# A hybrid encoder on one core: the recurrent mixer's score matmuls issued as one group, and the last cross-attention head's halves of the tokens in the other order

## The chip, the core and the metric

The kernel runs on one core of a Trainium2 chip, as one program. The metric is device time in microseconds of one execution. The core has a matrix engine (TensorE, PE in the views, with its weight loads as PEld), a vector engine (VectorE, DVE), an activation engine (ScalarE, ACT), a general engine (GpSimd, POOL) and SyncE (SP), which issues DMAs. Each engine works through its own stream of instructions in order; semaphores tie the streams together. SBUF is the on-chip working memory, PSUM holds the results of matmuls in eight banks of 128 × 512 float32.

## What is computed

Two layers over 1024 tokens of width 1024, all in float32. Each layer is a token mixer and a ConvGLU feed-forward, each between norms. Layer 0 mixes with windowed attention, layer 1 with a gated linear recurrence that runs forwards and backwards. Both mixers carry four cross-attention heads into 256 memory tokens. The part that the change touches, from the reference:

```python
def gla_chunked(q, k, v, log_f):            # one direction; chunks of HG_CHUNK tokens
    b = jnp.cumsum(log_f, axis=2)
    b_end = b[:, :, -1:]
    q_dec = q * jnp.exp(b)
    k_dec = k * jnp.exp(-b)
    k_end = k * jnp.exp(b_end - b)
    s = jnp.where(causal, jnp.einsum('bcthk,bcshk->bchts', q_dec, k_dec), 0.0)
    o_intra = jnp.einsum('bchts,bcshv->bcthv', s, v)
    def step(state, inp):
        qd, ke, vc, dec = inp
        o = jnp.einsum('bthk,bhkv->bthv', qd, state)
        state = dec[..., None] * state + jnp.einsum('bshk,bshv->bhkv', ke, vc)
        return state, o
...
    o = (gla_chunked(q, k_f, v, lf_f)
         + flip_t(gla_chunked(flip_t(q), flip_t(k_b), flip_t(v), flip_t(lf_b))))
    o = rmsnorm(o, norm_g.reshape(HG_HEADS, HG_VAL_DIM)).reshape(bsz, t, HG_W).astype(u.dtype)
    o = o * jax.nn.silu(gate)
    return jnp.concatenate([o, memory_cross_attn(xq, mem_kv)], axis=-1) @ w_out
```

There are 8 heads with keys and values of 128.

## The kernel before

**Stages.** `build` runs in this order: memory K/V for both layers and the first norm; `window` (layer 0's mixer); the output projection `WOut(0)`; `ffn(0)`; `hgrn` (layer 1's mixer); `WOut(1)`; `ffn(1)`. Every large product is three matmuls (`mm3`, `mmk`) on operands split into a high and a low part.

**Who sets the order.** The program is written with a framework whose planner decides, ahead of time, in which order each engine's instructions stand and which buffer a tile gets, from a simulated run of its own. Its preference is the order in which the kernel's code is written. `tc.high_priority(AHEAD)` lets what is written in its block rank as if it had been written `AHEAD` = 2000 instructions earlier. `tc.issue_after(ins)` puts the instructions of its block that run on the same engine behind `ins` in that engine's stream, without a wait for its end. On the chip each engine then follows its fixed stream.

**The recurrent mixer.** For each of the 8 heads `proj` makes q, the two forget inputs and, for two heads at a time, values and gates: long runs of projection matmuls into two PSUM banks (tag `pj`), 24 matmuls (8 input blocks, three each) for a bank. `head` then treats four directions: forwards over the first half of the tokens (d, b) = (0, 0), backwards over the second (1, 1), forwards over the second (0, 1), backwards over the first (1, 0). In the written order the projections of head h come before its directions and those of head h + 1 behind them.

`direction` makes decay factors on ScalarE, VectorE and GpSimd, with five buffers for the 128 × 512 tiles of tag `E` (E1, E2, and G for levels 32 and 64 among them) and two each for EP and ER. Scores within a 128-token chunk are made at three levels of blocks by `block` (line 1119): a matmul with 128 keys contracted, 32 stationary columns, 32 or 64 moving columns, and a place of its own among the array's columns. A direction has 8 calls at the 64-token level, 16 within blocks of 32 and 8 at the level of 32. `issue_after` puts the 24 others behind the first 8. All write the bank `pa[d]`. Behind them `copy_predicated` (line 1155) takes the valid scores out of `pa`, which go to As (line 1159 or 1161); ER is transposed (1164), copied to kT (1166), multiplied with v into the bank `pu` (1169), and the state S takes three or four steps on VectorE (1178) out of `pu`. The bank tags `po` and `pu` have one buffer each, `pt` has two.

`output` (for b = 1, then b = 0) sums scores times values and queries times states in `po` (1193), takes the mean square (line 100, ScalarE) and the root (line 93, GpSimd), scales into `on` (1199), transposes (1203), copies to `ot` (1205) and stores to `oT` in DRAM (1206).

**Cross-attention.** `cross` takes units (head, half of the tokens) from the list `units`, in places set by `HX`: two units each in heads 2, 4 and 6, behind the third and fourth direction, and in head 7 behind the second and third direction. The first unit of a head calls `cross_head`, which loads its keys and values and its query weights. `cross_unit` projects the query into `pj`, makes scores in `pt`, normalises, transposes, and accumulates the result in the bank `tags["po"][b]`: `po` for b = 0, `pu` for b = 1. It copies to `xo` (line 223), a tile that shares its one buffer with `ot`, and stores to `oT` from ScalarE's queue (224).

**The output projection** of layer 1 takes the token tiles in the order 4, 5, 6, 7, 0, 1, 2, 3. In head 7, behind the third direction's units, `wo1.early` begins tiles 4 and 5 with the heads that are done, in the two `pj` banks; `wo1.open` adds the last cross heads (reads of `oT`, line 453, split on line 86 and 87) and `finish` the last two recurrent heads, then the other tiles.

Of the kernel before, what the change touches and what calls it, by code (L numbers as in the profile page):

```python
# [16 lines left out]
P = 128  # L17
# [26 lines left out]
AHEAD = 2000  # L44


def build(tc, A, out):
# [130 lines left out]
    def cross_head(l, h, wp, raw):  # L178
        kvh = wp.tile([P, 2, 256], F32R, tag="kvh", bufs=1, name="kvh")
        kvl = wp.tile([P, 2, 256], F32R, tag="kvl", bufs=1, name="kvl")  # L180
        nc.sync.dma_start(raw, kvd[l][h])
        split(kvh, kvl, raw)
        return *wunit(A["wxq"][l, h]), kvh, kvl
# [755 lines left out]
    def hgrn():  # L939
# [5 lines left out]
        V, G = [late.tile([P, 3, NT, P], F32, name=x) for x in ("v", "gs")]  # L945
# [123 lines left out]
        def direction(h, r, d, b, qin, S, As):  # L1069
# [3 lines left out]
            lt, er = (0, 1) if d else (1, 0)  # L1073

            def E():
                return early.tile([P, 512], F32, tag="E", bufs=5, name="E")
# [24 lines left out]
            E1, E2 = E(), E()  # L1101
# [15 lines left out]
            def block(c, i, j, x, y, n=32):  # L1117

                return pe.matmul(pa[i:i + 32, c, j:j + n], x[:, c * P + i:c * P + i + 32], y[:, c * P + j:c * P + j + n],
                                 start=True, stop=True, tile_position=(0, i))  # L1120

            def step(n):
                pl_, pe_, rl_, re_ = parts(n)[:4]
                e = 0 if d else n - 1
                nb = 512 // (2 * n)
                dve.tensor_tensor(re_, re_, bc(pl_[:, :, e:e + 1], [P, nb, n]), op=ALU.mult)
                dve.tensor_tensor(pl_, pl_, bc(pe_[:, :, e:e + 1], [P, nb, n]), op=ALU.mult)  # L1127

            for n in (32, 64):
                step(n // 2)  # L1130
                G = E()
# [3 lines left out]
                dve.tensor_tensor(ge, re_, ke, op=ALU.mult)  # L1135
                if n == 32:
                    G32 = G
            for c in range(4):
                for o in (0, 32):
                    mm = block(c, er * 64 + o, lt * 64, G, G, 64)  # L1140
            with tc.issue_after(mm.ins):
                for c in range(4):
                    for o in range(0, P, 32):
                        block(c, o, o, E2, E1)
                for c in range(4):
                    for o in (0, 64):
                        block(c, o + er * 32, o + lt * 32, G32, G32)
            step(64)
            dec = wp.tile([P, 4], F32, tag="dec", bufs=2, name="dec")
            e = 0 if d else P - 1  # L1150
# [54 lines left out]
            act.activation(ot, tp, AF.Identity, scale=bng[:, h:h + 1])  # L1205
            nc.sync.dma_start(oT[1][h, :, b * 512:(b + 1) * 512], ot.rearrange("p c t -> p (c t)"))

        units = [(h, b) for h in range(4) for b in range(2)]
        xhead = [None]

        def cross(n):
            def pair(kind, i):
                return [wp.tile([P, 512], F32R, tag=kind + c, bufs=1, name=kind + c) for c in "hl"]

            for _ in range(n):
                xh_, xb_ = units.pop(0)
                if xb_ == 0:
                    raw = early.tile([P, 512], F32, tag="E", bufs=5, name="kv")
                    xhead[0] = cross_head(1, xh_, wp, raw.rearrange("p (a b) -> p a b", a=2))
                cross_unit(1, xh_, xb_, xhead[0], wp, tags, wp, pair)  # L1220

        def head(h, r):
            qin = [wp.tile([P, T], F32, tag=f"qin{d}", bufs=1, name="qin") for d in range(2)]
            S = [wp.tile([P, NT, P], F32, tag=f"S{d}", bufs=1, name="S") for d in range(2)]
            As = [None, None]
            for i, (d, b) in enumerate(((0, 0), (1, 1), (0, 1), (1, 0))):
                direction(h, r, d, b, qin[d], S[d], As)
                if i < len(r["later"]):
                    r["run"](r["later"][i])
                cross(HX[h][i])  # L1230
                if h == 7 and i == 2:
                    wo1.early(psj, 2, es)
            if h == 7:
                early.release()
                es.release()
                eq.release()
                wo1.open(2, 0)
            for i, b in enumerate((1, 0)):
                output(h, r, b, qin, S, As)
                cross(HX[h][4 + i])  # L1240
# [44 lines left out]
    wo0.finish()  # L1285
    ffn(0, wo0, h2d, True, (0, 1), (0, 1))
    hgrn()
    wo1.finish()
    ffn(1, wo1, out, False, (1, 0), (1, 0))
# [83 lines left out]
```

## Time and profile before

| | |
|---|---|
| median of 3 runs | 2715.87 us (2713.88 to 2719.8) |
| the profiled execution | 2715.91 us |
| its span, first to last instruction | 2714.1 us |
| mean granted TensorE clock | 0.992 |

| us from the start | what runs | TensorE busy |
|---|---|---|
| 0 to 250 | memory K/V, first norm, layer 0's mixer | 230.25 |
| 250 to 500 | layer 0's mixer | 233.07 |
| 500 to 1250 | output projection and feed-forward of layer 0 | 745.36 |
| 1250 to 1300 | start of the recurrent mixer | 48.86 |
| 1300 to 1900 | recurrent mixer | 588.74 |
| 1900 to 2000 | its end, output projection of layer 1 | 90.52 |
| 2000 to 2500 | output projection, feed-forward of layer 1 | 495.52 |
| 2500 to 2714.1 | feed-forward of layer 1 | 206.41 |

How to read the rows that follow. A row of the timeline has the start and the duration in us, the engine, the line of the kernel, the operation, output<-inputs by the program's names, the shape, the number of merged instructions, and in brackets the idle time of the engine ahead of it with what ended it. Matmuls are pipelined and their ends are modelled, so successive durations overlap; starts tell the pace. A `block` call leaves two records, since its operands are plain float32. A row of the view by stretches has from:to, the length, each engine's busy time with its instructions in the order PE, PEld, DVE, ACT, POOL, the granted TensorE clock, the DMA engines' share and GB/s.

### The profile page before, as it was taken

To read this page: it belongs to the slowest core of one execution; us is meant where nothing else is said; L and a number is where in the kernel's file an instruction comes from. 1 tells how busy PE (TensorE), PEld (TensorE's weight loads), DVE (VectorE), ACT (ScalarE), POOL (GpSimd) and SP (SyncE) were. 2 spreads that over 40 slices of the span, in tenths; PEclk is the share of its full clock that TensorE was granted. 3 is DMA by queue.
4 is the path that set the end of the run, shared out by engine and by line. 5 is a ranking of instruction groups with operands and counts; after the bars stand their busy time and mean duration, and the time that the engine had idled before them with its cause. 6 is when DMAs were issued, how large, how long until landed. Compare 5 with 4: busy or idle time off the path is not lost. (4 is left out here: it accounts for less than half of the span.)

```text
span 2714.1 us, 39502 instructions
## 1 busy us (share of the span) xinstructions
PE 2638.7 (97%) x14496; PEld 2204.5 (81%) x14496; DVE 1828.5 (67%) x3042; ACT 1391.6 (51%) x2556; POOL 468.4 (17%) x520
## 2 busy tenths in 40 slices
PE   8999999999999999999999999999899999999998
PEld 7888887788888888887877888878688788888887
DVE  6588787678565565487695768769567756566447
ACT  6367667545444444454454545545454544444443
POOL 1231110211111100031132222212121111110013
PEclk9999999999999999999999999999999999999999
DMA  7683213667777757673243432111476777775666
GB/s 284 209 179 84 60 52 100 188 190 181 210 197 196 205 149 255 195 256 124 69 150 106 111 88 67 52 51 34 125 219 174 188 209 206 202 201 155 226 194 233
DMA packets 215316, 432.25 MB, mean 159 GB/s; under 512 B 20561, under 2 KB 77265, under 8 KB 209489
## 3 DMA queue, kind: packets, MB, share of 16 engines
q1 hardware_dynamic: 188128, 335.07, 38.3%
q0 software_dynamic: 24544, 90.19, 15.9%
q10 hardware_dynamic: 2448, 4.46, 0.4%
q8 instruction: 114, 1.87, 0.3%
q14 instruction: 82, 0.66, 0.1%
HBM read 335.79 MB, written 117.96 MB: 167 GB/s over the span
## 5 line engine op out<-in xcount | busy, mean ns | idle before, releaser
L87 DVE TENSOR_TENSOR wl<-st,wh 128x1024 fp32r<-128x1024 f32 (+1 forms) x238 | 262.6, 1110 | 326.7 <-ACT wh L86 321.6
L86 ACT CAST wh<-st 128x1024 fp32r<-128x1024 f32 (+1 forms) x238 | 222.5, 937 | 295.9 <-PE X L535 195.9
L81 PE MATMUL pj<-uh,wh 128*128 128x512 f32 x512 | 205.2, 401 | 6.3 <-DVE xl L87 2.5
L535 PE MATMUL X<-wl,wh 128*128 128x512 f32 x528 | 204.8, 390 | 0.3 <-DVE wl L87 0.3
L535 PE MATMUL X<-wh,wl 128*128 128x512 f32 x528 | 204.6, 389 | 0.0
L82 PE MATMUL pj<-ul,wh 128*128 128x512 f32 x512 | 202.7, 396 | 0.1
L83 PE MATMUL pj<-uh,wl 128*128 128x512 f32 x512 | 202.2, 395 | 0.0
L535 PE MATMUL X<-wh 128*128 128x512 f32 x528 | 198.8, 390 | 1.4 <-ACT c L908 1.1
L81 PE MATMUL pj<-wh,uh 128*128 128x384 f32 (+1 forms) x512 | 190.4, 373 | 0.4 <-DVE v L280 0.4
L82 PE MATMUL pj<-wl,uh 128*128 128x384 f32 (+1 forms) x512 | 186.4, 364 | 0.0
L83 PE MATMUL pj<-wh,ul 128*128 128x384 f32 (+1 forms) x512 | 186.3, 365 | 0.0
L77 DVE TENSOR_TENSOR wl<-st,wh 128x1024 fp32r<-128x1024 f32 (+1 forms) x92 | 119.0, 1301 | 23.3 <-ACT wh L76 22.8
L535 PE MATMUL V<-uh,wh 128*128 128x512 f32 x344 | 133.8, 389 | 0.0
L535 PE MATMUL V<-ul,wh 128*128 128x512 f32 x344 | 133.8, 389 | 0.0
L535 PE MATMUL V<-uh,wl 128*128 128x512 f32 x344 | 133.8, 389 | 0.0
L76 ACT CAST wh<-st 128x1024 fp32r<-128x1024 f32 (+1 forms) x99 | 100.1, 1016 | 50.8 <-PE pj L82 31.0
L81 PEld LDWEIGHTS pj<-uh,wh 128*128 128x128 f32 x512 | 97.4, 190 | 26.7 <-DVE xl L87 2.9
L535 PEld LDWEIGHTS X<-wh 128*128 128x128 f32 x528 | 99.1, 188 | 22.8 <-ACT c L908 1.5
L535 PEld LDWEIGHTS X<-wl,wh 128*128 128x128 f32 x528 | 99.1, 188 | 21.0 <-DVE wl L87 0.7
L535 PEld LDWEIGHTS X<-wh,wl 128*128 128x128 f32 x528 | 99.1, 188 | 20.7
L1134 POOL TENSOR_TENSOR E<-EP,q 128x256 f32<-128x256 f32 x64 | 49.2, 769 | 372.3 <-DVE EP L1127 280.3
L83 PEld LDWEIGHTS pj<-uh,wl 128*128 128x128 f32 x512 | 97.0, 189 | 19.6
(347 smaller groups left out, 7274.4 us busy)
## 6 DMA issues: line engine op xcount, KB each, us to landing
st<-hid SPq DMA_DIRECT2D x154, 256.0 KB, 3.1
st<-in_ffw_dram SPq DMA_DIRECT2D x108, 256.0 KB, 3.1
w2s<-in_ffw_dram POOLq DMA_DIRECT2D x24, 1024.0 KB, 7.9
st<-in_ffw_dram SPq DMA_DIRECT2D x46, 512.0 KB, 4.1
hid<-tt SPq DMA_DIRECT2D x88, 256.0 KB, 4.6
st<-w2s SPq DMA_DIRECT2D x88, 256.0 KB, 3.3
sx<-in_ffw_dram SPq DMA_DIRECT2D x84, 256.0 KB, 3.9
sy<-in_ffw_dram SPq DMA_DIRECT2D x42, 512.0 KB, 6.3
```

Source lines behind the costliest of these rows:

```text
L76: act.copy(h[:, :n], raw)
L77: (eng or dve).tensor_tensor(l[:, :n], raw, h[:, :n].bitcast(F32), op=ALU.subtract)
L81: pe.matmul(o, ah, bh, start=first, stop=False)
L82: pe.matmul(o, ah, bl, start=False, stop=False)
L83: pe.matmul(o, al, bh, start=False, stop=last)
L86: act.copy(h, src)
L87: dve.tensor_tensor(l, src, h.bitcast(F32), op=ALU.subtract)
L535: pe.matmul(o, x, y, start=new, stop=e, skip_group_check=not first)
L1134: pool.tensor_tensor(gl, pl_, ql, op=ALU.mult)
```

## The change

The three loops over `block` go into a `high_priority` block as they are, `issue_after` included. And head 3 of the cross-attention, the last, takes its two halves of the tokens in the order 1, 0; `cross` finds the first unit of a head by a change of the head's number, no longer by b = 0.

```diff
-            for c in range(4):
-                for o in (0, 32):
-                    mm = block(c, er * 64 + o, lt * 64, G, G, 64)
-            with tc.issue_after(mm.ins):
+            with tc.high_priority(AHEAD):
                 for c in range(4):
-                    for o in range(0, P, 32):
-                        block(c, o, o, E2, E1)
-                for c in range(4):
-                    for o in (0, 64):
-                        block(c, o + er * 32, o + lt * 32, G32, G32)
+                    for o in (0, 32):
+                        mm = block(c, er * 64 + o, lt * 64, G, G, 64)
+                with tc.issue_after(mm.ins):
+                    for c in range(4):
+                        for o in range(0, P, 32):
+                            block(c, o, o, E2, E1)
+                    for c in range(4):
+                        for o in (0, 64):
+                            block(c, o + er * 32, o + lt * 32, G32, G32)
...
-        units = [(h, b) for h in range(4) for b in range(2)]
-        xhead = [None]
+        units = [(h, b) for h in range(4) for b in ((1, 0) if h == 3 else (0, 1))]
+        xhead = [None, None]
...
-                if xb_ == 0:
+                if xhead[1] != xh_:
+                    xhead[1] = xh_
                     raw = early.tile([P, 512], F32, tag="E", bufs=5, name="kv")
                     xhead[0] = cross_head(1, xh_, wp, raw.rearrange("p (a b) -> p a b", a=2))
```

## The prediction

> **What bounds the kernel now.** I read the page first, then busy time by stretches, then the groups of the changed line, then the TensorE timeline around it.
>
> ```profile
> span 2714.1 us, 39502 instructions
> PE 2638.7 (97%) x14496; PEld 2204.5 (81%) x14496; DVE 1828.5 (67%) x3042; ACT 1391.6 (51%) x2556; POOL 468.4 (17%) x520
> ```
>
> TensorE is busy for 97% of the span; no other engine is above 67%. The next view has, for a stretch of time, its length and each engine's busy time (with its instructions), then the granted clock and the DMA share:
>
> ```profile
> 1300.00:1900.00 600.00, 588.74 (x4664) 488.49 (x4666) 449.48 (x902) 308.12 (x675) 152.12 (x166) 0.99 0.29 82
> ```
>
> This stretch is the body of the recurrent mixer. In it TensorE idles 600 − 588.74 = 11.3 us, with VectorE at 449.48 / 600 = 75%. So there the end is set by how long TensorE needs for its stream of instructions, and what shortens that stream shortens the span. The score matmuls (`block`, line 1119) are part of it:
>
> ```profile
> L1119 PE MATMUL pa<-E x2048: 192/196/243, 1278.0 to 1919.2; 128*32 128x32 f32 x140, 128*32 128x64 f32 x47
> ```
>
> That is 32 directions (8 heads, 4 each) of 32 calls, 64 records a direction since a call leaves two. In the TensorE timeline these 2048 records stand in 73 unbroken runs, of which these are the first and the last:
>
> ```profile
> 1278.04 0.41 PE L1119 MATMUL pa<-E 128*32 128x64 f32 x6
> ...
> 1918.52 0.83 PE L1119 MATMUL pa<-E 128*32 128x64 f32 x52
> ```
>
> 19 directions are one run of 64. The other 13 are cut into 5, 3, 7, 3, 6, 5, 3, 6, 5, 3, 4, 2 and 2 runs (54 together), so there are 54 − 13 = 41 runs more than directions. One of the directions in five pieces, with the matmuls at its seams:
>
> ```profile
> 1615.25 0.39 PE L83 MATMUL pj<-wh,ul 128*128 128x512 f32 x1
> 1615.57 0.76 PE L1119 MATMUL pa<-E 128*32 128x64 f32 x26
> 1616.26 0.50 PE L81 MATMUL pj<-wh,uh 128*128 128x512 f32 x1
> 1616.59 0.39 PE L82 MATMUL pj<-wl,uh 128*128 128x512 f32 x1
> 1616.82 0.40 PE L83 MATMUL pj<-wh,ul 128*128 128x512 f32 x1
> ...
> 1621.92 0.32 PE L1119 MATMUL pa<-E 128*32 128x32 f32 x12
> 1622.17 0.50 PE L81 MATMUL pj<-wh,uh 128*128 128x512 f32 x1
> ...
> 1627.84 0.27 PE L1119 MATMUL pa<-E 128*32 128x32 f32 x8
> 1628.03 0.50 PE L81 MATMUL pj<-wh,uh 128*128 128x512 f32 x1
> ...
> 1633.70 0.32 PE L1119 MATMUL pa<-E 128*32 128x32 f32 x8
> 1633.95 0.50 PE L81 MATMUL pj<-wh,uh 128*128 128x512 f32 x1
> ...
> 1639.62 0.38 PE L1119 MATMUL pa<-E 128*32 128x32 f32 x10
> 1639.92 0.66 PE L1164 MATMUL pt<-ident,ER 128*128 128x128 f32 x4
> ```
>
> The durations overlap, so starts are compared. Two projection matmuls in a row start 0.23 us apart (1616.59 to 1616.82). A run is entered 0.32 after the matmul before it (1615.25 to 1615.57), 0.09 more. The first projection matmul behind it holds the engine 0.33 (1616.26 to 1616.59), 0.10 more. So each run pays about 0.19 us at its seams, besides its own length, and a direction in pieces pays that for each piece. A whole direction:
>
> ```profile
> 1397.16 0.39 PE L83 MATMUL pj<-uh,wl 128*128 128x512 f32 x1
> 1398.98 1.17 PE L1119 MATMUL pa<-E 128*32 128x64 f32 x64 [1.44 <-DVE s L1041]
> 1400.08 0.50 PE L81 MATMUL pj<-uh,wh 128*128 128x512 f32 x1
> ```
>
> **The change part by part.** *The score matmuls under high priority.* No instruction is added or removed; the order on TensorE changes. A direction's 32 calls now rank before about 2000 earlier instructions, so the planner should issue them together as soon as the last input G is ready, not in the gaps of the projection's stream.
>
> Price of a cut, from the rows above. From the run's start to the next other matmul: 0.69 + 0.25 + 0.19 + 0.25 + 0.30 = 1.68 for the five pieces, 1.10 for the whole run (1398.98 to 1400.08). With seams: 1.68 + 5 × 0.19 = 2.63 against 1.10 + 0.19 = 1.29. Four cuts cost 1.34 us, 0.335 each. Lower end: the eight-record run takes 0.19 + 0.19 = 0.38, and eight records inside the whole run take 8 × 1.10 / 64 = 0.14, so 0.24 is lost. Upper end: all 0.38 is lost. For 41 cuts that is 9.8 to 15.6 us, with 41 × 0.335 = **13.7 us** as my value, since the five-piece direction is the commonest form. I let the whole of it come off the span, because the cuts lie in the stretch with 11.3 us of idle in 600. One of the 41, in the last direction, lies where TensorE also waits; it changes nothing within the bounds.
>
> *What moves with it.* The follow-up work (`copy_predicated` of line 1155, the copy or sum into As, the transposes of ER) keeps its rank but gets its input sooner. For the direction above the last G was ready at 1599.91 + 0.76 = 1600.67 and its last scores came at 1640.0:
>
> ```profile
> 1599.91 0.76 POOL L1134 TENSOR_TENSOR E<-EP,q 128x256 f32<-128x256 f32 x1 [1.04 <-DVE EP L1127]
> ```
>
> E1, E2 and the two G tiles then come free up to 39 us sooner, which lets the next direction's ScalarE and VectorE work start. Its cost to TensorE is nothing while projection matmuls fill the time; if that cover is gone, TensorE would wait. The gain can't be more than the 11.3 us of idle in the body; the loss is the stall rival below. I take 0.
>
> *Second half of the tokens first.* The head's two units are the same instructions in the other order. The K/V load, the weight load and their split go to whichever unit is first, so no DMA is added; the two stores on ScalarE's queue change places. The unit for b = 1 accumulates in the bank `pu` and that for b = 0 in `po`, so the banks change places in time too. The end of the mixer now:
>
> ```profile
> 1914.89 1.16 PE L1169 MATMUL pu<-v,kT 128*128 128x128 f32 x8
> 1919.29 0.49 PE L1193 MATMUL po<-v,As 128*128 128x128 f32 x2
> 1930.41 1.79 PE L1169 MATMUL pu<-v,kT 128*128 128x128 f32 x8 [2.28 <-ACT xo L223]
> 1933.41 0.79 PE L1193 MATMUL po<-S,qin 128*128 128x128 f32 x2 [1.21 <-DVE S L1178]
> 1947.08 0.50 PE L81 MATMUL pb<-wh,oh 128*128 128x512 f32 x1 [0.54 <-ACT ot L1205]
> ```
>
> ```profile
> 1917.92 0.59 ACT L223 COPY xo<-po 128x512 f32<-128x512 f32 x1 [3.08 <-PE po L83]
> 1929.78 0.58 ACT L223 COPY xo<-pu 128x512 f32<-128x512 f32 x1
> 1938.17 0.40 ACT L86 CAST oh<-or 128x256 fp32r<-128x256 f32 x1 [1.51 <-DMA or<-oT]
> ```
>
> ```profile
> 1925.62 1.13 DVE L1199 SCALAR_TENSOR_TENSOR on<-po,ors,gs 128x128 f32<-128x128 f32 x4 [1.13 <-POOL ors L93]
> 1943.82 1.13 DVE L1199 SCALAR_TENSOR_TENSOR on<-po,ors,gs 128x128 f32<-128x128 f32 x4 [0.90 <-POOL ors L93]
> ```
>
> Today the last direction's `pu` waits 2.28 us for the second unit's copy (1929.78), and the state step behind it 1.21 more. Those waits go: the second unit will hold `po`. Late next is `output(b=1)`, which needs `po`. If it queues behind the unit, it starts at 1930.4 instead of 1919.29. It needs 1919.29 to 1926.75 = 7.5 us until `on` frees the bank, so 1937.9; the second output needs 7.5 again, or 1933.41 to 1944.95 = 11.5 as today, so 1945.4 to 1949.4; today's 1944.95 to 1947.08 = 2.1 behind it gives 1947.5 to 1951.5, that is 0.4 to 4.4 us later than 1947.08. If output(b=1) gets the bank first, as it does in time today, the unit's copy stays near 1929.8, the last `pu` no longer waits, and the second output runs 1930.4 to 1937.9, the next stage at 1940: 7 us sooner. The direction before, whose `pu` ran at 1914.89, waits for the first unit's copy (1918.5), 3.6 us, which the bank wait covers. For it, the tokens that the output projection reads first are stored a unit sooner, so ScalarE's cast of 1938.17 no longer waits 1.51 us for its load. Range −7 to +4.4. Banks are most likely handed out in the program's order, where the loss is nearer its lower price of 0.4 (7.5 us was measured without a load in ScalarE's way); the load wait saved is about as much, so I take **0**.
>
> **Sum**, against the profiled execution (2715.9 us, span 2714.1; the median of the runs is 2715.9 too): 2715.9 − 13.7 + 0 + 0 = **2702 us**.
>
> **The rivals.** *Stalls (slower).* TensorE issues in order. A group put ahead of the projections at the moment the planner believes G is ready holds up everything behind it if G is late on the chip: all projection matmuls, and through the two `pj` banks the next q and s. The row at 1398.98 is such a case, 1.44 us of idle. It decides from 13.7 / 13 = 1.05 us for each of the 13 regrouped directions. With 1.44 each: 18.7 − 13.7 = +5 us. And a pause can cost clock: behind 1.90 us of idle the clock in the records falls.
>
> ```profile
> 1902.49 0.50 PE L83 MATMUL pb<-wh,oe 128*128 128x512 f32 x1 [1.90 <-DVE oe L87]
> ```
>
> ```profile
> 1903.50:1906.90 3.40, 3.40 (x9) 2.56 (x8) 3.40 (x7) 1.64 (x3) 1.70 (x1) 0.51 0.69 192
> ```
>
> Half of 3.4 us, 1.7, is lost there. Were that so behind half of the 13, another 11 us: 2716 + 5 + 11 = **2732**. Against it: of the 19 whole groups, already issued soon after their inputs, only this one shows idle ahead of it. Chance 0.11. The Trainium skill (TensorE: Matmul & The Clock Gate, "Why this matters for your kernels") asks only that pauses stay under about 3 us; by that no stall of 1.44 would touch the clock and the case would end at 2721. The row at 1903.5, half clock behind 1.90 us, differs from it, and the row decides.
>
> *Idle time goes too (faster).* Earlier scores, earlier free tiles: half of the 11.3 us of idle goes, and the end gains part of its 7: 2702 − 6 − 4 = **2692**. For it stands the 39 us of lateness above; against it, that the idle is small pieces. Chance 0.16.
>
> *The swap costs its 4.4 and cuts are cheap:* 2716 − 9.8 + 4.4 = **2710**. Chance 0.08.
>
> *Nothing arrives:* other work still cuts in, or VectorE's chain (75% busy) turns the saved time into waits for s and q: **2715**. Chance 0.09; against it, TensorE's 98% in the body.
>
> **How the numbers follow.** My forecast has the remaining 0.56, by itself 2697 to 2708. A difference of 0.2%, 5.4 us, is about what a measurement of this kernel tells from none. Faster: 0.56 + 0.16 + 0.08 = 0.80; same: 0.09; slower: 0.11. The range 2689 to 2714 leaves out the stall and half of "nothing arrives".
>
> **What would show it.** Runs of line 1119: 32 or few more instead of 73, each near 1.1 us to the next matmul. TensorE's busy time down by some 13 us, its idle in the mixer's body near 11 us. Idle ahead of line 1119 with VectorE or GpSimd as releaser would show the stall; a long wait of line 1193 for `xo` would show the swap's price. Wrong would be: runs whole and the span unchanged, or projections waiting more for s and q.

## The result and the profile after

| | before | after |
|---|---|---|
| median of 5 runs each | 2715.87 us (2711.23 to 2719.8) | 2703.28 us (2700.27 to 2705.6) |
| ratio | | 0.9954, 95% interval 0.994 to 0.9967 |
| the profiled execution | 2715.91 us | 2705.6 us |
| its span | 2714.1 us | 2703.8 us |

The forecast was 2702 us. Below the changed block the lines of the changed kernel are one higher than before (`pu` 1170, the state step 1179, `output` 1194, `on` 1200); 1119, 1134 and 223 stay. The head of the page and the busy time by engine, for the changed kernel:

```profile
span 2703.8 us, 39480 instructions
PE 2626.8 (97%) x14496; PEld 2202.5 (81%) x14496; DVE 1835.5 (68%) x3042; ACT 1397.5 (52%) x2556; POOL 469.3 (17%) x520
```

TensorE is busy for 2638.7 − 2626.8 = 11.9 us less, with the same 14496 instructions. The scores, in the TensorE timeline of the changed kernel:

```profile
1586.53 0.39 PE L1194 MATMUL po<-S,qin 128*128 128x128 f32 x2
1586.85 1.17 PE L1119 MATMUL pa<-E 128*32 128x64 f32 x64
1587.94 0.49 PE L1194 MATMUL po<-S,qin 128*128 128x128 f32 x2
```

Each direction is now one row of 64 records, 32 such rows in all. A direction is entered 0.32 us behind the matmul before it and left after 1587.94 − 1586.85 = 1.09 us, as the whole directions were before.

Where the time went is seen by cutting the mixer in three at the same events in both kernels: from the mixer's first projection matmul to the first `pb` matmul (the **body**), from there to the last transposes of `on` (the **tail**), and the rest up to the first matmul of layer 1's feed-forward. The view by stretches, first of the kernel before; the rows are body, tail and whole mixer:

```profile
1234.95:1894.55 659.60, 646.78 (x4944) 534.60 (x4943) 490.89 (x980) 332.89 (x722) 162.74 (x182) 0.99 0.29 83
1894.55:1945.37 50.82, 41.87 (x328) 33.64 (x326) 36.29 (x81) 23.34 (x63) 11.93 (x12) 0.90 0.38 114
1234.95:2068.78 833.83, 810.63 (x5833) 669.27 (x5832) 602.29 (x1172) 418.63 (x901) 194.93 (x215) 0.99 0.34 101
```

And of the changed kernel:

```profile
1239.20:1877.11 637.91, 628.08 (x4930) 527.99 (x4928) 501.55 (x977) 337.04 (x722) 165.60 (x181) 1.00 0.30 86
1877.11:1934.99 57.88, 44.32 (x340) 34.94 (x338) 37.99 (x86) 25.26 (x66) 11.32 (x12) 0.88 0.33 105
1239.20:2058.02 818.82, 794.53 (x5834) 664.40 (x5832) 611.12 (x1173) 425.01 (x905) 196.00 (x215) 0.99 0.34 103
```

The body is 659.60 − 637.91 = 21.7 us shorter, much more than the 13.7 forecast; the tail is 57.88 − 50.82 = 7.1 us longer, where the forecast had 0; the rest is 0.4 shorter. That makes 15.0 for the mixer. The span gained only 10.3, mainly because the stretch ahead of the mixer, whose work is the same in both kernels, took 1239.20 us in this execution against 1234.95 (what follows the mixer took 0.4 more). Over the 14 profiles of this document that first stretch took 1235.0 to 1241.4 us, so single executions are compared below by their mixer and kernels by their medians.

In the body TensorE's idle time fell from 659.60 − 646.78 = 12.8 to 9.8 us, and the granted clock from 0.99 came to 1.00: by the clock's records, 6.8 us of the body before were at half clock (3.4 us lost), and none after. So the 21.7 are 3.0 of idle, 3.4 of clock and 15.3 of work at full clock. Part of what the last has over the forecast is 14 matmuls that crossed the mark into the tail (4944 to 4930); but a kernel below (e3) has 15.1 with none crossing, so the split is good to an us or two. Over the whole mixer, the length less idle time less half of the half-clock time (I call it **net work**) went from 802.1 to 787.7, that is 14.4 us.

The waits of TensorE, before:

```profile
PE pu L1169 <- ACT kT L1166: 4.4, 3, 1.5
PE pb L81 <- ACT oh L86: 3.7, 4, 1.3
...
PE pu L1169 <- ACT xo L223: 2.3, 1, 2.3
```

and after (total us, times, longest):

```profile
PE pb L81 <- ACT oh L86: 9.0, 5, 3.9
PE pa L1119 <- POOL E L1134: 4.4, 4, 1.6
```

In the body, three waits of `pu` for kT, 4.4 us, went, and four waits of the scores for G came, 4.4 us as well. What fell on balance there are waits for q and s, from 5.2 to 1.0 us, against 2.2 us of new waits for the gates `gs`. In the tail the wait for `xo` went, as the prediction said, and the output projection waits for `oh` 9.0 us instead of 3.7; all of this increase is in the tail. What is late behind the swap is in the next rows of the changed kernel, ScalarE, TensorE and VectorE:

```profile
1903.30 0.59 ACT L223 COPY xo<-pu 128x512 f32<-128x512 f32 x1 [2.46 <-PE pu L83]
...
1915.80 0.59 ACT L223 COPY xo<-po 128x512 f32<-128x512 f32 x1
```

```profile
1916.53 0.41 PE L1194 MATMUL po<-v,As 128*128 128x128 f32 x2
...
1925.06 0.39 PE L1194 MATMUL po<-v,As 128*128 128x128 f32 x2
...
1931.62 0.79 PE L81 MATMUL pb<-xwh,oh 128*128 128x512 f32 x1 [3.93 <-ACT oh L86]
```

```profile
1923.45 1.12 DVE L1200 SCALAR_TENSOR_TENSOR on<-po,ors,gs 128x128 f32<-128x128 f32 x4
...
1931.94 1.12 DVE L1200 SCALAR_TENSOR_TENSOR on<-po,ors,gs 128x128 f32<-128x128 f32 x4
```

`output(b=1)` starts at 1916.53, right behind the copy that empties `po` (1915.80 + 0.59 = 1916.39). It is the queue for the bank that the prediction named as the swap's price.

### The profile page after: what moved, and what is told of

Read it like the earlier page. It is cut to its first block, busy times and chain, and to the rows that moved or that the text cites. A ratio compares the mean times of both kernels' runs of the same rounds, so it can differ in the third digit from the quotient of the medians.

```text
span 2703.8 us, 39480 instructions
## 1 busy us (share of the span) xinstructions
PE 2626.8 (97%) x14496; PEld 2202.5 (81%) x14496; DVE 1835.5 (68%) x3042; ACT 1397.5 (52%) x2556; POOL 469.3 (17%) x520
## 5 line engine op out<-in xcount | busy, mean ns | idle before, releaser
L535 PEld LDWEIGHTS X<-wh 128*128 128x128 f32 x528 | 99.1, 188 | 24.3 <-ACT c L908 3.0
L81 PEld LDWEIGHTS pj<-uh,wh 128*128 128x128 f32 x512 | 96.9, 189 | 24.3 <-DVE xl L87 2.9
L82 PEld LDWEIGHTS pj<-ul,wh 128*128 128x128 f32 x512 | 97.0, 189 | 18.6 <-DVE ul L87 0.4
```

The source lines that it names most:

```text
L81: pe.matmul(o, ah, bh, start=first, stop=False)
L82: pe.matmul(o, ah, bl, start=False, stop=False)
L535: pe.matmul(o, x, y, start=new, stop=e, skip_group_check=not first)
```

## The experiments

The same accounting for every kernel, from one profiled execution each; the medians are against the kernel before on the same chip in the same job. "Cuts" are runs of line 1119 beyond 32. Half clock comes in steps of 3.4 us in these records, and one step is 1.7 us of time. A pause inside such a stretch is taken off one and a half times, so net work is good to about an us: the ten profiles without cuts give 787.5 to 789.6.

| kernel | cuts | mixer, us | idle | at half clock | net work | median less that of before, us | ratio (95%) |
|---|---|---|---|---|---|---|---|
| before | 41 | 833.8 | 23.2 | 17.1 | 802.1 | | |
| changed | 0 | 818.8 | 24.3 | 13.7 | 787.7 | −12.6 | 0.9954 (0.994–0.9967) |
| e1, block alone | 0 | 817.5 | 21.5 | 17.1 | 787.5 | −21.1 | 0.9923 (0.9909–0.9937) |
| e6, the same again | 0 | 813.8 | 21.4 | 6.8 | 789.0 | −21.1 | 0.9924 (0.9912–0.9937) |
| e2, swap alone | 41 | 837.4 | 28.6 | 13.7 | 802.0 | +2.4 | 1.0012 (1.0003–1.0021) |
| e3, whole but late | 0 | 818.5 | 23.8 | 13.7 | 787.8 | −11.3 | 0.9953 (0.9941–0.9965) |
| e4, banks in order | 0 | 812.2 | 20.9 | 3.4 | 789.6 | −17.6 | 0.993 (0.9917–0.9942) |
| e10, the same again | 0 | 817.3 | 23.5 | 10.2 | 788.7 | −17.6 | 0.9935 (0.9922–0.9947) |
| e5, changed again | 0 | 819.8 | 22.1 | 20.5 | 787.5 | −14.6 | 0.9943 (0.9931–0.9956) |
| e9, changed, third | 0 | 818.9 | 22.7 | 17.1 | 787.8 | −13.0 | 0.9955 (0.9942–0.9967) |
| e7, heads 0 to 3 | 49 | 836.8 | 24.5 | 13.7 | 805.5 | +4.3 | 1.0014 (1.0005–1.0023) |
| e8, first 8 calls | 50 | 829.6 | 18.4 | 13.7 | 804.4 | −6.8 | 0.9977 (0.9968–0.9986) |
| e11, units earlier | 0 | 819.9 | 25.0 | 13.7 | 788.1 | −13.4 | 0.9948 (0.9935–0.9962) |
| e12, and banks | 0 | 818.9 | 24.1 | 13.7 | 788.0 | −14.2 | 0.995 (0.9937–0.9962) |

**Each part alone (e1, e2).** e1 keeps the high-priority block and takes the units in the old order:

```diff
-        units = [(h, b) for h in range(4) for b in ((1, 0) if h == 3 else (0, 1))]
+        units = [(h, b) for h in range(4) for b in range(2)]
```

> The high-priority block alone; the cross head keeps its order 0, 1. Seam theory (each of the 41 cuts cost TensorE about 0.335 us, and the swap is worth about nothing): some 13.7 us below before, near 2702, with 32 runs of line 1119, and TensorE's time from the mixer's first projection to the last feed-forward, less its idle time and half of its half-clock time, down by 13 to 15 us. If the swap costs its priced 0.4 to 4.4 us in the mixer's end, this kernel is that much faster than the changed one, 2698 to 2703; if the swap gains, it is slower than the changed one by up to 7 us, up to 2710.

e2 is the kernel before with the edit of `units` and `xhead` alone:

```diff
-        units = [(h, b) for h in range(4) for b in range(2)]
-        xhead = [None]
+        units = [(h, b) for h in range(4) for b in ((1, 0) if h == 3 else (0, 1))]
+        xhead = [None, None]
...
-                if xb_ == 0:
+                if xhead[1] != xh_:
+                    xhead[1] = xh_
```

> The order 1, 0 of the last cross head alone; the score matmuls keep their 73 runs. Seam theory: within 5 us of before, 2711 to 2721. If the swap costs its 0.4 to 4.4 us: 2716 to 2720, with output(b=1) starting only behind the second unit's copy of xo, some 10 us later against the last scores than in before. If the swap is what brought the gain: 2703 to 2709.

The block alone took 2697.95 against 2719.04 us, 21.1 us less; the swap alone 2721.41, 2.4 more (0.8 to 5.7 by its interval). Together they should have given 18.7; the changed kernel gave 12.6, 14.6 and 13.0 in its three comparisons. So neither term taken as 0 is 0, they have opposite signs, and the swap costs more where the scores are early. The end of the mixer with the swap alone, on ScalarE, TensorE and VectorE:

```profile
1929.88 0.58 ACT L223 COPY xo<-po 128x512 f32<-128x512 f32 x1
```

```profile
1930.60 0.41 PE L1193 MATMUL po<-v,As 128*128 128x128 f32 x2
...
1939.04 0.39 PE L1193 MATMUL po<-v,As 128*128 128x128 f32 x2
```

```profile
1937.43 1.12 DVE L1199 SCALAR_TENSOR_TENSOR on<-po,ors,gs 128x128 f32<-128x128 f32 x4
...
1946.00 1.12 DVE L1199 SCALAR_TENSOR_TENSOR on<-po,ors,gs 128x128 f32<-128x128 f32 x4
```

The prediction's loss case had `output(b=1)` at 1930.4, its `on` done at 1937.9 and the second output done at 1945.4 to 1949.4. Here they stand at 1930.60, 1937.43 + 1.12 = 1938.55 and 1946.00 + 1.12 = 1947.12 (this mixer began 1.0 us later than the one before). That case came about to within a microsecond.

**Block alone and changed kernel on one chip (e5, e6).** e5 is the changed kernel and e6 is e1 once more.

> The changed kernel once more, on the same chip as the next run. If the swap costs 4 us of idle time in the mixer's end (as the first profiles say: 13.6 us of idle there against 9.9 without it), it is 3 to 8 us above the regrouped kernel without the swap; if the two are alike and the earlier difference was that between chips, within 2 us of it.

> The high-priority block alone, once more, beside the changed kernel: 17 to 22 us below before if the first result holds, of which some 14 are net TensorE time (787.5 us in the mixer against 802.1) and the rest less idle time and fewer half-clock windows in the mixer's body; 13 to 15 us below if the seams are all there is.

2703.82 against 2697.28 us: on top of the block the swap costs 6.5 us. The end of the mixer in e6, by the same three engines and the view by stretches (body, tail):

```profile
1900.28 0.59 ACT L223 COPY xo<-po 128x512 f32<-128x512 f32 x1 [2.52 <-PE po L83]
...
1911.66 0.60 ACT L223 COPY xo<-pu 128x512 f32<-128x512 f32 x1
```

```profile
1901.73 0.38 PE L1194 MATMUL po<-v,As 128*128 128x128 f32 x2
...
1912.31 1.16 PE L1170 MATMUL pu<-v,kT 128*128 128x128 f32 x8 [0.96 <-ACT xo L223]
1915.54 0.79 PE L1194 MATMUL po<-S,qin 128*128 128x128 f32 x2 [2.07 <-DVE S L1179]
```

```profile
1907.90 1.12 DVE L1200 SCALAR_TENSOR_TENSOR on<-po,ors,gs 128x128 f32<-128x128 f32 x4
...
1922.79 1.13 DVE L1200 SCALAR_TENSOR_TENSOR on<-po,ors,gs 128x128 f32<-128x128 f32 x4 [1.19 <-POOL ors L93]
```

```profile
1236.20:1873.91 637.71, 628.10 (x4929) 527.96 (x4928) 501.85 (x977) 337.08 (x722) 164.41 (x181) 1.00 0.30 86
1873.91:1925.11 51.20, 40.31 (x331) 32.20 (x330) 36.72 (x84) 23.93 (x64) 11.35 (x12) 0.93 0.33 106
```

The body is that of the changed kernel (637.71 to 637.91 us), the tail 6.7 us shorter (51.20 against 57.88; 53.6 in e1's profile). In the old order `output(b=1)` takes `po` at 1901.73, behind the first unit, and runs while the second unit works in `pu`; its `on` is done before that unit is. With the swap it starts behind the second unit. The last direction's waits for `xo` and for the state are there, 0.96 and 2.07 us, as they were before.

Why 6.5 here and 2.4 with the late scores? The second output is counted from its start (in the old order, from the row that waits for the state) to the end of its `on`. In the kernel before it took 1943.82 + 1.13 − 1933.41 = 11.5 us, with the swap alone 1947.12 − 1939.04 = 8.1: what the queue delayed, it gave back in part. With the block alone it took only 1923.92 − 1915.54 = 8.4 (8.0 in e1), in the changed kernel 1933.06 − 1925.06 = 8.0, so there was next to nothing to give back. ScalarE's stream shows where the 11.5 come from. In the kernel before, between the squares of the second output (line 100), stands a cast that waits for its load:

```profile
1941.10 0.41 ACT L86 CAST oh<-or 128x256 fp32r<-128x256 f32 x1 [1.86 <-DMA or<-oT]
```

In e6, e1, e2 and the changed kernel no cast with a wait stands between them. So the length of the second output seems to go with where the planner puts such a cast. Late scores alone don't make it long: in e7 below, whose last heads have late scores and the old order, it took 8.5 us. This is read from single profiles and was not tested.

**Whole but late (e3).** The first call keeps its old rank and pulls the other 31 behind it in one piece; units in the old order. Against the kernel before:

```diff
-            for c in range(4):
-                for o in (0, 32):
-                    mm = block(c, er * 64 + o, lt * 64, G, G, 64)
-            with tc.issue_after(mm.ins):
+            g = [(c, o) for c in range(4) for o in (0, 32)]
+            mm = block(0, er * 64, lt * 64, G, G, 64)
+            with tc.high_priority(AHEAD), tc.issue_after(mm.ins):
+                for c, o in g[1:]:
+                    block(c, er * 64 + o, lt * 64, G, G, 64)
...
```

> No swap. The first score matmul of a direction keeps its natural rank, so it still waits for a gap in the projections; the 31 others follow it at high priority, so the group is whole but as late as in before. Seam theory: the same gain as the block under high priority, near 2702, with TensorE's net time in the mixer down by 13 to 15 us. Rival (the gain comes from scores that are ready sooner, and so from idle time that goes): near before, 2712 to 2718, with the net time unchanged.

All 41 cuts are gone and the net work is 787.8, as with the early groups, but the median is 2707.73 against e1's 2697.95 on the same chip. Wholeness gives the net work; earliness gives the rest. ("Late" is against the block: direction 25 of the 32, for one, has its scores 512 us into the mixer in e6, 536 in e3, and from 547 to 571 before.) The body, its first stretch at half clock, and a wait beside it:

```profile
1237.78:1885.06 647.28, 633.37 (x4944) 531.94 (x4942) 491.75 (x983) 333.28 (x725) 167.33 (x183) 0.99 0.30 85
...
1654.80:1661.60 6.80, 5.84 (x14) 4.64 (x15) 5.69 (x16) 1.02 (x4) 3.18 (x4) 0.50 0.00 0
```

```profile
1655.76 0.80 PE L81 MATMUL pj<-uh,wh 128*128 128x512 f32 x1 [3.78 <-DVE xl L87]
```

Idle is 647.28 − 633.37 = 13.9 us against 9.6 in e6. Two waits for `xl`, VectorE's split of a cross-attention input, make up 3.78 and 4.38 of it, and 10.2 us of the body are at half clock: 6.8 that begin late in this wait, and 3.4 that begin late in the other (1825.4). In VectorE's stream `xl` (1655.02) stands behind the copy of a direction's scores out of `pa` (1646.22) and the next direction's decay factors, which fill most of the time between. Body against body, 647.3 − 637.7 = 9.6 us is what earliness is worth beside this late version; beside the kernel before it is the 6.4 of idle and clock found above.

**Banks in time order (e4).** The changed kernel, with the last cross head's units in the banks the other way round, so that the first unit has `po` again:

```diff
-        po = tags["po"][b]()
+        po = tags["po"][1 - b if l and h == 3 else b]()
```

> The changed kernel, but the last cross head's first unit accumulates in po and its second in pu, as in before, although the first unit now treats the second half of the tokens. If the wait of output(b=1) for the second unit's copy is what lengthens the end of the mixer, that wait goes, the last pu waits for the copy again as in before (2 to 3 us), and the time is 2 to 6 us below the changed kernel, 2697 to 2701. If the bank isn't what ends last there: within 2 us of the changed kernel.

**On one chip with the changed kernel (e9, e10).** e9 is the changed kernel, e10 is e4 again.

> The changed kernel, on the same chip as the next three: 13 to 16 us below before.

> The changed kernel with the last head's banks in the order of time (first unit po, second pu). Bank theory: the second output's scaling (on) ends some 687 us behind the mixer's first projection, as without the swap, and not 694 as in the changed kernel; the time is 3 to 7 us below the changed kernel. If the earlier store of the second half of the tokens were worth something by itself, it would also be below the kernel without the swap, by its 1.5 us of load wait.

2699.98 against 2704.64 us: 4.7 us come back when the order of the tokens stays swapped and only the bank changes (e4: 17.6 against 12.6 below before, 5.0). The last `pu` waits for the copy again, 1.0 us in e4 and 0.8 in e10. The tail is 50.1 us in e10 and 50.5 in e4, against 57.9, 58.8 and 57.9 in the three profiles of the changed kernel. So at least most of the swap's cost is the bank's; by the medians 1.8 to 3.5 us of it don't come back, which the overlapping intervals don't tell from nothing (0.993 and 0.9935 against 0.9923 and 0.9924 for the block alone). For the same reason the stores that come earlier show no gain. The expected end of the second `on`, some 687 us into the mixer, came in e4 (687.0) but not in e10 (690.7), whose body was 4.1 us longer in this profile, with one stretch at half clock.

**Half of the heads (e7) and the first eight calls (e8).** Both keep the units in the old order. e7 raises heads 0 to 3 alone:

```diff
-            with tc.high_priority(AHEAD):
+            with tc.high_priority(AHEAD if h < 4 else 0):
```

> No swap; high priority for heads 0 to 3 alone, and heads 4 to 7 at their natural rank. The planner cuts those last 16 directions into 65 pieces, so there are 81 runs, 49 cuts. Seam theory at 0.35 us a cut: TensorE's net time in the mixer 787.6 + 17 = some 805 us, up to 3 above before with its 41 cuts, so the time is near before or above it, 2716 to 2724. If the price hangs on the neighbour (many of these pieces stand between transposes, not projections): net 797 to 802. Rival (earlier scores bring the gain): a third to a half of the regrouped kernel's gain, 2708 to 2714, net near 788 to 795.

e8 raises the 8 calls at the 64-token level and leaves the other 24 at their rank (against the kernel before):

```diff
-            for c in range(4):
-                for o in (0, 32):
-                    mm = block(c, er * 64 + o, lt * 64, G, G, 64)
+            with tc.high_priority(AHEAD):
+                for c in range(4):
+                    for o in (0, 32):
+                        mm = block(c, er * 64 + o, lt * 64, G, G, 64)
             with tc.issue_after(mm.ins):
...
```

> No swap; only the first 8 of a direction's 32 calls have high priority, the other 24 keep their natural rank. They start early but end late, in 82 runs, 50 cuts. Seam theory: net time 787.6 + 17.5 = some 805 us, and a time of 2717 to 2725, slower than before. Rival (an early start brings the gain): faster than before, 2708 to 2714.

One direction in e8 begins like this in the TensorE timeline, its first 8 calls whole (16 records) and projection matmuls between the rows:

```profile
1597.88 0.64 PE L1119 MATMUL pa<-E 128*32 128x64 f32 x16
1606.16 0.33 PE L1119 MATMUL pa<-E 128*32 128x32 f32 x16
1612.54 0.26 PE L1119 MATMUL pa<-E 128*32 128x32 f32 x4
```

Both kernels have more cuts than before, 49 and 50, and both have more net work, 805.5 and 804.4. Against 788.2, the mean of the ten profiles without cuts, a cut costs 17.3 / 49 = 0.35 and 16.2 / 50 = 0.32 us, and in the kernel before 13.9 / 41 = 0.34. The times don't follow the net work alone: e7 is 4.3 us slower than before, e8 is 6.8 us faster. Cut in the middle of the mixer's projection matmuls, e7's body shows both halves of its edit; the first and second half of the body in the kernel before, in e7, and the first half in e6:

```profile
1234.95:1559.04 324.09, 315.33 (x2354) 258.88 (x2352) 235.25 (x462) 159.40 (x338) 83.51 (x97) 0.99 0.36 108
1559.04:1894.55 335.51, 331.45 (x2594) 275.72 (x2593) 255.64 (x520) 173.49 (x385) 79.22 (x85) 0.99 0.21 59
```

```profile
1240.29:1552.44 312.15, 307.13 (x2353) 256.97 (x2352) 245.71 (x472) 165.46 (x347) 83.45 (x98) 1.00 0.39 115
1552.44:1899.95 347.51, 340.46 (x2569) 278.91 (x2568) 250.12 (x499) 168.78 (x370) 83.16 (x84) 0.99 0.19 53
```

```profile
1236.20:1548.34 312.14, 307.23 (x2354) 256.99 (x2353) 245.96 (x473) 165.77 (x347) 83.44 (x98) 1.00 0.39 116
```

In the first half, where its heads are raised, e7 gains 11.9 us, as much as e6; in the other, which has all its 49 cuts, it loses 12.0. The idle time that goes is in the first half too (8.8 to 5.0 us). In e8's mixer the idle time is 18.4 us, the least of all, against 23.2; the view by stretches has it whole:

```profile
1235.36:2064.97 829.61, 811.20 (x5833) 667.95 (x5832) 604.56 (x1172) 418.10 (x903) 201.31 (x215) 0.99 0.34 101
```

The mixer is 4.2 us shorter than before in spite of nine more cuts (833.83 − 829.61). So a theory of cuts alone falls on e8, while its price for a cut holds in all three.

**Units earlier (e11, e12).** To have both units of the last cross head out of the way, they go behind the first and second directions of head 7; e11 with the old order, e12 with the swap and e4's banks:

```diff
-HX = [(0,) * 6, (0,) * 6] + [(0, 0, 1, 1, 0, 0), (0,) * 6] * 2 + [(0, 0, 1, 1, 0, 0), (0, 1, 1, 0, 0, 0)]
+HX = [(0,) * 6, (0,) * 6] + [(0, 0, 1, 1, 0, 0), (0,) * 6] * 2 + [(0, 0, 1, 1, 0, 0), (1, 1, 0, 0, 0, 0)]
```

> High-priority block without the swap, and the last head's two units one direction earlier (behind the first and second direction of head 7, not the second and third). If the end of the mixer is set by the chain second unit, bank pu, last direction, second output, it shortens: the wait of about 1 us for xo ahead of the last pu goes, and some of the 10 us of TensorE's idle time there: 2 to 5 us below the kernel without it. If the units only change places with other work that the end waits for, within 2 us of it.

> The same with the changed order of the halves and the banks in the order of time. Expected within 2 us of the run before it, if the order of the halves by itself is worth nothing.

2704.18 and 2703.41 us: slower than the block alone by 7 to 8 us, compared by way of the kernel before, where 2 to 5 us faster was expected of e11; the two are within 2 us of each other, as expected. In e11's profile `on` of the first output was ready 684.5 us into the mixer, against 672.8 in e6. The TensorE timeline shows the first output breaking off and going on 15 us later; the last row is ScalarE's:

```profile
1903.81 0.39 PE L1194 MATMUL po<-v,As 128*128 128x128 f32 x2
...
1916.47 1.76 PE L1170 MATMUL pu<-v,kT 128*128 128x128 f32 x8
1918.67 0.71 PE L1194 MATMUL po<-S,qin 128*128 128x128 f32 x4 [0.44 <-DVE S L1179]
```

```profile
1915.83 0.58 ACT L223 COPY xo<-pu 128x512 f32<-128x512 f32 x1 [1.18 <-PE pu L83]
```

The first output goes on when the third direction's states are there; their `pu` starts at 1916.47, right behind the copy that takes the second unit out of that bank (1915.83 + 0.58 = 1916.41). In e6 that direction's `pu` ran ahead of the second unit (1898.84). So moving the units earlier seems to have made another queue for a single bank; this is read from the timeline and no further run shows it.

The lowest ratio is the block alone's, 0.9923 and 0.9924 of the time before; it isn't clear of e4's.

## Why the prediction came out right

The total was right (2702 against 2703.28 us) and so was its largest term, but two terms of the sum were wrong and largely cancelled: the block alone gains 21.1 us, 7 more than forecast, and the swap takes 6.5 back. That the total fits this closely is luck.

**The cuts: 41 × 0.335 = 13.7 us.** Right. Measured net work fell by 14.4 us (802.1 to 787.7), and the price came out at 0.32 to 0.35 us in three kernels with 41, 49 and 50 cuts. The later whole groups of e3 give the same net work as the early ones, so this term is the price of the cuts, however early the scores are.

**"What moves with it": 0.** Wrong in size; the direction was among the bounds. It was held that TensorE's cost and gain are nothing while projection matmuls fill the time, with a gain of at most the 11.3 us of idle. The idle of the body fell by 3.0 us in the changed kernel: waits for kT, q and s went, new ones for G and the gates took part of it back. And 3.4 us of clock came with it, a cost that the prediction had priced for stalls to come, not for those already there: in the kernel before two of the three waits for kT were followed by half clock. That the early place and not the wholeness brings this is shown by e3 against e1 (9.8 us on one chip) and by e8, which is faster with more cuts. How the gain divides between idle and clock rests on single profiles.

**"Second half of the tokens first": 0, range −7 to +4.4.** Wrong in the choice within its range. The place was as put: the last `pu` no longer waits, and `output(b=1)` queues for `po` behind the second unit. By itself it costs 2.4 us (e2). The 0 came from two steps: that the loss would lie near its lower price of 0.4, and that the load wait saved would pay for it. The bank's order (e4, e10) returns at least most of the cost and the earlier stores show no gain. On top of the early scores it costs 6.5 us (e5 against e6), above the upper end. That end was worked out from the end of the mixer as it was, where the second output takes 11.5 us; in the profiles with the other half of the change it takes 8.0 to 8.4, and less of the delay is given back.

**The rivals.** *Idle time goes too* was half right: its body came about (21.7 us measured, 13.7 + 6 forecast), its gain at the end turned into the swap's loss. *The swap costs its 4.4 and cuts are cheap* had the right mechanism for the swap, with cuts at the wrong price. *Stalls* came in 4 of 32 groups, 4.4 us in all by the row of waits for G, below its break-even of 1.05 us for each of 13; none was followed by half clock in the changed kernel. *Nothing arrives* fell with the shorter body.

**What was to show it.** 32 runs of line 1119: yes. TensorE's busy time down by some 13: 11.9. Idle in the body near 11, that is unchanged: it fell, from 12.8 to 9.8 in the body as cut here. A long wait of the output matmuls for `xo`: not as a row of waits, because the planner had other matmuls stand ahead of them; it showed as the position of `output(b=1)` in the stream, and as 9.0 us of waits of `pb` for `oh`. A queue for a buffer that a planner foresees is found in the order of starts, not among the waits.

## What to carry to other kernels

Where one engine is busy 98% of the time, count how often its long streams are broken and price a break by comparing starts across a broken and a whole group; times the count, that gave the net work here to within some 5%, and two thirds of the time that the block gained. An edit that makes work whole also moves it, so look up the waits that its later steps end today (here `pu` for kT, and the half clock behind), and give that gain a number. Two edits in one change are priced in the order in which they take effect: the second against the profile that the first leaves, and a swap of two units by which single-buffer bank each holds and who needs that bank next.

## What the runs showed of the hardware

**Half clock behind short pauses, but not behind all.** In the kernel before, a pause of 1.46 us on TensorE was followed by a stretch at half clock; first the timeline's row, then the view by stretches:

```profile
1496.52 1.43 PE L1169 MATMUL pu<-v,kT 128*128 128x128 f32 x8 [1.46 <-ACT kT L1166]
```

```profile
1497.30:1500.70 3.40, 3.40 (x14) 3.05 (x13) 3.40 (x7) 2.61 (x7) 0.00 (x0) 0.50 0.97 200
```

Pauses of 1.29 and 0.34 us stood shortly before it. The same wait of `pu` in a later head, 1.45 us at 1664.73, left the clock whole; that of 1.47 us at 1831.43 was followed by half clock from 1831.8 us on. In the changed kernel a pause of 1.61 us left it whole as well:

```profile
1462.97 1.17 PE L1119 MATMUL pa<-E 128*32 128x64 f32 x64 [1.61 <-POOL E L1134]
```

```profile
1463.00:1470.00 7.00, 7.00 (x92) 5.99 (x93) 3.78 (x11) 1.22 (x3) 4.90 (x5) 1.00 0.42 77
```

So the length of a single pause doesn't decide it; what does was not tried. The Trainium skill (TensorE: Matmul & The Clock Gate, "Why this matters for your kernels") asks that pauses stay under about 3 us. The 1.46 us here, and the 1.90 us shown in the prediction, stayed under it and still lost clock; the 3.78 us of e3 lies over it and lost clock.
